# Hybrid layer on one core: delta-rule key factor by reciprocal, values' turns last, head norms run within the next head, memory K/V projected token-major with 512 moving columns

## The chip, the cores and the metric

The kernel runs on one core of a Trainium2 chip. The metric is the device time of one execution in microseconds (us); a kernel is run several times and the median is given. Engines are named as in the profile: PE multiplies matrices (PEld loads its stationary operand), DVE, ACT and POOL work on tiles, SP issues DMAs.

## What is computed

One step of a layer for 512 prompt tokens and 64 sample tokens (T = 576) with a model width of 1024. Everything is fp32, and the batches share the weights:

```python
h = x + concat(gdn, diff) @ w_out          # both from proj = rmsnorm(x) @ w_in
h = h + mem_attn(rmsnorm(h), mk, mv, w_mem_q, w_mem_o)
h = h + square(relu(rmsnorm(h) @ w_ff1)) @ w_ff2
y = rmsnorm(h)
# delta rule: k, q normed to length 1; chunks; unit lower triangular solve
ka = ka * rsqrt(sum(ka * ka) + EPS)
# diff attention, per head: two softmaxes, then a norm of the head's output
a = p[:, :, 0] - lam * p[:, :, 1]
ob = rmsnorm(a @ v, diff_norm) * (1 - lam_init)
# memory of the prompt: 256 tokens, 4 heads of 256
m = rmsnorm(mem, ln_mem_kv)
mk, mv = m @ w_mem_k, m @ w_mem_v          # both are outputs too
```

Outputs are y for both batches, the new keys and values of attention and memory, the delta rule's state and the convolution's last rows. The sample tokens use caches for the attention's and the memory's keys and values.

## The kernel before

**Products.** A large projection is done in a split format: x and w are each a high part in fp32r and a rest, and each product is three matmuls (wh·xh, wh·xl, wl·xh). `weights` (L141) loads 128 columns of a weight as raw tiles (three buffers), and ACT (L147) and DVE (L148) make `wh` and `wl` (two buffers each). `project` (L151) keeps a 128x128 piece of the weight stationary and moves 256 or 320 columns of the transposed activations through it; the result lies feature-major in one PSUM bank `pr` (three of them). The other banks are `ba` (two), `g0`, `g1` and `gs` (one each).

**Order.** A scheduler places the instructions on each engine by priorities that follow the program's order, and each engine runs its own list in order. Independent matmuls, here called filler, so come to stand between dependent ones: projections of the next stage within the delta rule and within the attention. A tile with few buffers is reused only when its readers are done.

**Stages.** The input projection and convolution; the delta rule in four chunks of 128 and one of 64; the attention, four heads with five query tiles each; the memory's K and V; `w_out`; the memory attention; the feed-forward layers `w_ff1` and `w_ff2`; the last norm.

**Delta rule.** `gdn_prep` prepares a chunk c with one bank, g0 or g1 by c's parity, through which everything goes in turn: the turns of the keys `bk` and of the queries `bq`; POOL's power of −1/2 of the sums of squares s8 (L527, `rpow` at L174); from it `nk` (L529), `brk` (L530, L531) and `rq2`; the turns `bv` of the values, scaled by `nk` into `vb` (L534 to L538); the decay `bg` (a matmul of `triu` and `gg`), the products `bkk` and `bkq`, and from L571 on the solve: `At` is made of `bkk`, `brk` and the decay, X is turned, and six levels of small products follow. `gdn_scan` then applies the chunk.

**Attention.** `diff_project` makes queries, keys and values of a head and writes the keys out through a staging tile `ko`, which shares its buffers with the probabilities `p0`. `diff_head` runs five query tiles (the sample's, t = 4, comes first). Behind them the head's norm: sums `so`, POOL's power `co` (L804), the product `an` on DVE (L805), five turns on PE, two scaled copies on ACT (L811) into `od`.

**Memory K/V (L824 to L844).** Eight weights each of 128 columns: feature-major products of 256 tokens, a copy, two turns, and copies into a staging tile `tm` (for K; it shares its buffers with `p1`), from which K goes out, or into `mv`.

**Row broadcast.** `norm_columns` gets a token's norm factor as a column (POOL's power at L884); `row_broadcast` (L176) turns the columns into rows by matmuls with the identity, and copies them to `rB`, which scales the results of the next projection.

## Time and profile before

| | |
|---|---|
| median of 3 runs | 1105.75 us (1105.25 to 1108.7) |
| profiled execution | 1104.43 us |
| its span | 1102.7 us |
| granted clock of PE, mean | 0.986 |
| stage 40 to 180 us: length, PE busy | 140.0, 134.82 us |
| stage 516 to 628 us: length, PE busy | 112.0, 108.66 us |
| DMA over the span | 90.62 MB, 82 GB/s |

The span runs from the first to the last instruction in the trace; what the execution takes besides is 1.7 us. In the views below a line such as `PE g L98 <- DVE vb L538` reads: PE, at an instruction of line 98 that writes a tile g, waited for DVE's writing (or reading) of `vb` at line 538. `pr<-u,wh 128*128 128x256` is an operation with its output, its inputs and its shapes; x3 is a count. Times of instructions on PE overlap, so what a matmul costs is the distance from one start to the next.

### The profile page before, as it was taken

The page shows a single profiled execution, that of the slowest core. Times are in us where ns is not written, and L with a number is a line of the kernel's source. Part 1 is how long each engine was busy: PE and PEld are TensorE (multiplying, and loading weights), DVE is VectorE, ACT ScalarE, POOL GpSimd, SP SyncE. Part 2 cuts the span into 40 slices and gives each one's busy share as a digit, 9 for nine tenths or more (in the row PEclk, how much of TensorE's full clock was granted, in tenths as well). Part 3 has the DMA queues.
Part 4 walks back from the last instruction along what each step waited for, and adds up shares of the span by engine and source line. Part 5 has one row for each costly group of instructions (what it writes and reads, how often), then busy time and mean ns, then how long its engine had stood idle before and what let it go on. Part 6 is the DMA issues. An engine that isn't in the chain of part 4 may idle for free.

```text
span 1102.7 us, 18954 instructions
## 1 busy us (share of the span) xinstructions
PE 1056.7 (96%) x7708; PEld 1002.8 (91%) x7708; DVE 623.8 (57%) x1335; ACT 408.4 (37%) x842; POOL 78.6 (7%) x127
## 2 busy tenths in 40 slices
PE   5999899899999999899999999999999999999997
PEld 5999799888888888799988799999999999999996
DVE  6766674665455566355454555655555555455554
ACT  5533554233135557543332343322222222222244
POOL 5421120221000000000000000000000000000000
PEclk9999999999999999899999999999999999999998
DMA  7242310100122254434211032223323141414122
GB/s 220 84 141 71 117 39 21 41 20 12 48 78 60 91 171 118 134 117 151 69 47 39 23 93 78 59 72 92 86 77 96 58 116 49 115 50 114 58 78 86
DMA packets 151494, 90.62 MB, mean 82 GB/s; under 512 B 5472, under 2 KB 147934, under 8 KB 150896
## 3 DMA queue, kind: packets, MB, share of 16 engines
q1 hardware_dynamic: 151408, 89.41, 27.6%
q8 instruction: 61, 1.00, 0.4%
q14 instruction: 25, 0.20, 0.1%
HBM read 79.66 MB, written 9.74 MB: 81 GB/s over the span
## 4 chain that ended last, share of the span: by engine, by line
issue 41%; PE 30%; DVE 1%; DMA 1%; ACT 1%; POOL 1%; POOLq 0%; ACTq 0%; SPq 0%
PE pr L98 20%; PE g L98 4%; PE ba L102 3%; PE gs L98 2%; PE ba L98 2%; DMA out_dram<-p 1%; POOL ta L174 0%; DVE an L805 0%; POOL tiny L174 0%; PE g L102 0%; DVE u L998 0%; ACT p L840 0%; DVE wl L148 0%; POOLq L1031 0%; ACT p L927 0%
## 5 line engine op out<-in xcount | busy, mean ns | idle before, releaser
L98 PE MATMUL pr<-u,wh 128*128 128x256 f32 (+1 forms) x3936 | 811.5, 300 | 0.4
L98 PEld LDWEIGHTS pr<-u,wh 128*128 128x128 f32 x3936 | 638.2, 191 | 7.0 <-issue 2.0
L98 PE MATMUL pr<-u,wl 128*128 128x256 f32 (+1 forms) x1968 | 584.9, 298 | 0.0
L98 PEld LDWEIGHTS pr<-u,wl 128*128 128x128 f32 x1968 | 373.2, 190 | 1.3 <-issue 0.2
L147 ACT CAST wh<-raw 128x1024 fp32r<-128x1024 f32 (+1 forms) x161 | 141.4, 878 | 289.0 <-PE pr L98 266.2
L148 DVE TENSOR_TENSOR wl<-raw,wh 128x1024 fp32r<-128x1024 f32 (+1 forms) x161 | 163.0, 1012 | 66.5 <-ACT wh L147 62.2
L858 DVE TENSOR_TENSOR u<-u,pr 128x256 f32<-128x256 f32 (+1 forms) x160 | 72.4, 453 | 105.2 <-PE pr L98 105.2
L964 DVE TENSOR_TENSOR p<-pr,rB 128x256 f32<-128x256 f32 x64 | 29.3, 458 | 65.4 <-PE pr L98 65.4
L167 ACT CAST u<-p 128x256 fp32r<-128x256 f32 x64 | 27.8, 434 | 89.2 <-DVE p L965 87.5
L174 POOL TENSOR_TENSOR tiny<-tiny,nhalf 128x1 f32<-128x1 f32 (+2 forms) x10 | 10.3, 1032 | 658.7 <-DVE tiny L882 488.3
L168 DVE TENSOR_TENSOR u<-p,u 128x256 fp32r<-128x256 f32 x64 | 29.2, 457 | 20.2 <-ACT u L167 20.2
L98 PE MATMUL g<-u,qz 128*128 128x256 f32 (+4 forms) x96 | 29.2, 405 | 1.2 <-ACT p L781 1.2
L965 DVE SCALAR_TENSOR_TENSOR p<-p 128x256 f32<-128x256 f32 x64 | 29.3, 458 | 1.7
L102 PE MATMUL ba<-ident,u 128*128 128x128 f32 (+2 forms) x128 | 22.7, 318 | 6.0 <-ACT p L840 3.2
L355 DVE SCALAR_TENSOR_TENSOR p<-p,gcol,p 128x579 f32<-128x579 f32 x33 | 27.1, 820 | 0.9
L98 PE MATMUL g<-Dt,B 128*128 128x128 f32 (+1 forms) x200 | 26.6, 278 | 0.9 <-DVE B L571 0.9
L571 DVE SCALAR_TENSOR_TENSOR B<-lev,At 128x512 f32<-128x512 f32 (+1 forms) x30 | 20.9, 708 | 10.0 <-PE g L98 6.9
L98 PEld LDWEIGHTS g<-Dt,B 128*128 128x128 f32 (+1 forms) x200 | 22.7, 185 | 4.0 <-ACT X L602 2.9
L781 ACT ACTIVATE p<-g,ta 128x320 f32<-128x320 f32 (+4 forms) x40 | 21.2, 532 | 13.6 <-DVE ta L779 10.4
L98 PE MATMUL g<-Y,X 128*128 128x128 f32 (+1 forms) x192 | 25.6, 274 | 0.2
L602 ACT COPY X<-g 128x512 f32<-128x512 f32 (+1 forms) x24 | 13.2, 549 | 33.7 <-PE g L102 33.6
L170 ACT ACTIVATE u<-u,gcol 128x256 fp32r<-128x256 f32 (+1 forms) x32 | 17.1, 533 | 23.1 <-DVE u L858 23.1
(270 smaller groups left out, 981.6 us busy)
## 6 DMA issues: line engine op xcount, KB each, us to landing
raw<-in_w_ff_dram SPq DMA_DIRECT2D x32, 512.0 KB
raw<-in_w_ff_dram SPq DMA_DIRECT2D x64, 256.0 KB
raw<-in_w_in_dram SPq DMA_DIRECT2D x28, 512.0 KB
raw<-in_w_mem_k_dram SPq DMA_DIRECT2D x8, 512.0 KB
raw<-in_w_mem_v_dram SPq DMA_DIRECT2D x8, 512.0 KB
raw<-in_w_out_dram SPq DMA_DIRECT2D x8, 512.0 KB
raw<-in_w_mem_q_dram SPq DMA_DIRECT2D x8, 512.0 KB
raw<-in_w_mem_o_dram SPq DMA_DIRECT2D x8, 512.0 KB
```

The lines of the kernel that those rows point to most:

```text
L98: nc.tensor.matmul(out, lhsT, rhs, start=start, stop=stop)
L102: nc.tensor.transpose(out, in_, ident[:n, :n])
L147: A.copy(wh, raw)
L148: V.tensor_tensor(wl, raw, wh.bitcast(F32), ALU.subtract)
L167: A.copy(h, src)
L168: V.tensor_tensor(lo, src, h.bitcast(F32), ALU.subtract)
L355: V.scalar_tensor_tensor(yv[:, :n], cb[:, i : i + n], cwt[:, m, i : i + 1], yv[:, :n], ALU.mult, ALU.add)
L571: V.scalar_tensor_tensor(B[:n, :, :n], lev[:n, :n].unsqueeze(1).to_broadcast([n, 4, n]), float(lv), At[:n, :, :n], ALU.is_equal, ALU.mult,)
L781: A.activation(p[:, :nk], b[:, :nk], AF.Exp, bias=mx[:, c : c + 1], scale=0.125, accum_out=l[:, c : c + 1])
L858: V.tensor_tensor(hm, hm, b, ALU.add)
L964: V.tensor_tensor(f, b, rB[:, a0 : a0 + n], ALU.mult)
L965: V.scalar_tensor_tensor(f, f, 0.0, f, ALU.max, ALU.mult)
```

## The change

There are four edits. (1) In `gdn_prep` the key factor `brk` is DVE's reciprocal of the sum of squares, times beta, in place of the square of POOL's power; `nk`, `rq2`, the turns of the values and `vb` move behind the product `KQ`. (2) `diff_head` returns its norm as a function `finish`, which the next head runs ahead of its third query tile, t = 1; the last head's runs behind the loop. (3) Memory K and V are made token-major: a 128x128 piece of the memory's tokens is stationary and 512 columns of the weight move, two banks `pr` for a block of 512 features; a raw tile holds 256 rows of the weight by 512 columns. Copies of DVE (tokens 0 to 127) and ACT (the rest) go to `mkt` (a tile of its own, unit 7) or `mv`, from which the outputs leave; only K is turned, from `mkt` into `mkT`. (4) The row broadcast runs between the two halves of the first projection that uses it, and two of its matmuls are kept in program order.

The diff, with most of its context left out; the end of it does to ff1 what is shown of the memory queries:

```diff
@@ -94,8 +94,10 @@
-    def mm(out, lhsT, rhs, start=True, stop=True):
-        nc.tensor.matmul(out, lhsT, rhs, start=start, stop=stop)
+    def mm(out, lhsT, rhs, start=True, stop=True, pin=False):
+        i = nc.tensor.matmul(out, lhsT, rhs, start=start, stop=stop)
+        if pin:
+            tc.keep_in_program_order(i)
@@ -138,17 +140,21 @@
 
-    def weights(w, c0, kt=KT):
-        raw = load(w, c0, kt)
-        wh = wp.tile([P, kt, P], F32R, tag="wh", name=nm("wh"))
-        wl = wp.tile([P, kt, P], F32R, tag="wl", name=nm("wl"))
+    def split_weights(w, shape):
+        raw = wp.tile(shape, F32, tag="raw", name=nm("raw"), bufs=3)
+        nc.sync.dma_start(raw, w.rearrange("(k p) n -> p k n", p=P))
+        wh = wp.tile(shape, F32R, tag="wh", name=nm("wh"))
+        wl = wp.tile(shape, F32R, tag="wl", name=nm("wl"))
         with tc.high_priority():
 
-    def project(w, x, evac, kt=KT, halves=HALVES):
+    def weights(w, c0, kt=KT):
+        return split_weights(w[:, c0 : c0 + P], [P, kt, P])
+    def project(w, x, evac, kt=KT, halves=HALVES, between=None):
 
@@ -158,6 +164,8 @@
+            if between and a0 == 0:
+                between()
@@ -173,16 +181,16 @@
 
-    def row_broadcast(rst, ntok, out):
+    def row_broadcast(rst, ntok, out, pin=False):
 
         for t in range(full):
-            mm(b[:, t * P : (t + 1) * P], bc(rst[:, t : t + 1], [P, P]), ident)
+            mm(b[:, t * P : (t + 1) * P], bc(rst[:, t : t + 1], [P, P]), ident, pin=pin and t == 0)
         A.copy(out[:, : full * P], b[:, : full * P])
             b2 = bank()
-            mm(b2[:, :DEC], bc(rst[:DEC, 4:5], [DEC, P]), ident[:DEC, :DEC])
+            mm(b2[:, :DEC], bc(rst[:DEC, 4:5], [DEC, P]), ident[:DEC, :DEC], pin=pin)
             V.tensor_copy(out[:, full * P :], b2[:, :DEC])
@@ -525,17 +533,9 @@
         rpow(r8[:n], s8[:n])
-        nk, brk, rq2 = tiny([P, 4], "tg"), tiny([P, 4], "tg"), tiny([P, 4], "tg")
-        V.tensor_tensor(nk[:n], s8[:n, 0:4], r8[:n, 0:4], ALU.mult)
-        V.tensor_tensor(brk[:n], r8[:n, 0:4], r8[:n, 0:4], ALU.mult)
+        brk = tiny([P, 4], "tg")
+        V.reciprocal(brk[:n], s8[:n, 0:4])
         V.tensor_tensor(brk[:n], brk[:n], beta[:n, c, :], ALU.mult)
-        V.tensor_scalar(r8[:n, 4:8], r8[:n, 4:8], P ** -0.5, None, ALU.mult)
-        V.tensor_tensor(rq2[:n], r8[:n, 4:8], r8[:n, 4:8], ALU.mult)
-        bv = bank(f"g{c % 2}")
-        for h in range(H):
-            tr(bv[:n, h * P : (h + 1) * P], cv_[:, h, L])
-        vb = sb("vb")
-        V.tensor_tensor(vb[:n], v4(bv, P)[:n], nk[:n].unsqueeze(2).to_broadcast([n, 4, P]), ALU.mult)
 
@@ -560,6 +560,15 @@
         V.tensor_tensor(KQ[:n, :, :n], v4(bkq, n)[:n], gam[:n, :, :n], ALU.mult)
+        nk, rq2 = tiny([P, 4], "tg"), tiny([P, 4], "tg")
+        V.tensor_tensor(nk[:n], s8[:n, 0:4], r8[:n, 0:4], ALU.mult)
+        V.tensor_scalar(r8[:n, 4:8], r8[:n, 4:8], P ** -0.5, None, ALU.mult)
+        V.tensor_tensor(rq2[:n], r8[:n, 4:8], r8[:n, 4:8], ALU.mult)
+        bv = bank(f"g{c % 2}")
+        for h in range(H):
+            tr(bv[:n, h * P : (h + 1) * P], cv_[:, h, L])
+        vb = sb("vb")
+        V.tensor_tensor(vb[:n], v4(bv, P)[:n], nk[:n].unsqueeze(2).to_broadcast([n, 4, P]), ALU.mult)
         if c > 0:
@@ -754,13 +763,15 @@
 
-    def diff_head(h):
+    def diff_head(h, between):
 
         for t in (4, 0, 1, 2, 3):
+            if t == 1:
+                between()
             q0 = QT[t][0]
@@ -800,48 +811,62 @@
             A.copy(on[:, t, :], po)
-        V.tensor_scalar(so, so, 1.0 / P, EPS, ALU.mult, ALU.add)
-        rpow(co, so)
-        V.tensor_tensor(on, on, co.unsqueeze(2).to_broadcast([P, 5, P]), ALU.mult)
-        b, b2 = bank(), bank()
-        for t in range(4):
-            tr(b[:, t * P : (t + 1) * P], on[:, t, :])
-        tr(b2[:, :P], on[:, 4, :])
-        for src, ts_ in ((b, slice(0, SEQ)), (b2[:, DEC:P], slice(SEQ, T))):
-            A.activation(od[:, h, ts_], src, AF.Identity, scale=dn)
+        def finish():
+            V.tensor_scalar(so, so, 1.0 / P, EPS, ALU.mult, ALU.add)
+            rpow(co, so)
+            V.tensor_tensor(on, on, co.unsqueeze(2).to_broadcast([P, 5, P]), ALU.mult)
+            b, b2 = bank(), bank()
+            for t in range(4):
+                tr(b[:, t * P : (t + 1) * P], on[:, t, :])
+            tr(b2[:, :P], on[:, 4, :])
+            for src, ts_ in ((b, slice(0, SEQ)), (b2[:, DEC:P], slice(SEQ, T))):
+                A.activation(od[:, h, ts_], src, AF.Identity, scale=dn)
+        return finish
+    finish = lambda: None
     for h in range(H):
             diff_cache()
-        diff_head(h)
+        finish = diff_head(h, finish)
+    finish()
 
 
-    mxs = ([mh[:, 0:4, :], mh[:, 4:8, :]], [ml[:, 0:4, :], ml[:, 4:8, :]])
     mkT = unit(2, [P, KT, NMEM])
     mv = unit(3, [P, 2, D])
-    for w, out in ((w_mem_k, o_mk), (w_mem_v, o_mv)):
-        for m in range(KT):
-            d = mkT[:, m, :] if out is o_mk else small("zr", [P, 320])[:, :NMEM]
-            project(weights(w[0], m * P), mxs, lambda b, a0, n: A.copy(d, b), halves=((0, NMEM),))
-            b = bank()
-            for bi in range(2):
-                tr(b[:, bi * P : (bi + 1) * P], d[:, bi * P : (bi + 1) * P])
+    mkt = unit(7, [P, 2, D])
+    for w, dst, out in ((w_mem_k, mkt, o_mk), (w_mem_v, mv, o_mv)):
+        for f in range(2):
+            fs = slice(512 * f, 512 * f + 512)
+            bs = [bank("pr") for _ in range(2)]
+            for kc in range(4):
+                wt = split_weights(w[0, 256 * kc : 256 * kc + 256, fs], [P, 2, 512])
+                for k in (2 * kc, 2 * kc + 1):
+                    for t in range(2):
+                        ts_ = slice(t * P, (t + 1) * P)
+                        for j, (wi, x) in enumerate(((0, mh), (0, ml), (1, mh))):
+                            mm(
+                                bs[t], x[:, k, ts_], wt[wi][:, k % 2, :],
+                                start=(k == 0 and j == 0), stop=(k == KT - 1 and j == 2),
+                            )
+            for t in range(2):
+                (A.copy if t else V.tensor_copy)(dst[:, t, fs], bs[t])
             if out is o_mk:
-                if m % 2 == 0:
-                    tm = small("tm", [P, 2, 256])
-                dst = tm[:, :, (m % 2) * P : (m % 2 + 1) * P]
-            else:
-                dst = mv[:, :, m * P : (m + 1) * P]
-            A.copy(dst, b[:, :256].rearrange("p (b n) -> p b n", b=2))
-            if out is o_mk and m % 2:
-                nc.sync.dma_start(out[0, 0, :, m // 2, :].rearrange("(b p) d -> p b d", p=P), tm)
-        if out is o_mv:
-            nc.sync.dma_start(out[0, 0].rearrange("(b p) h d -> p b (h d)", p=P), mv)
+                for i in range(2):
+                    b = bank()
+                    for j in range(2):
+                        m = 4 * f + 2 * i + j
+                        for t in range(2):
+                            tr(b[:, j * 256 + t * P : j * 256 + (t + 1) * P], dst[:, t, m * P : (m + 1) * P])
+                    m = 4 * f + 2 * i
+                    A.copy(mkT[:, m : m + 2, :], b.rearrange("p (j n) -> p j n", j=2))
+            nc.sync.dma_start(out[0, 0].rearrange("(b p) h d -> p b (h d)", p=P)[:, :, fs], dst[:, :, fs])
 
@@ -890,7 +915,8 @@
-    rB = row_broadcast(norm_columns(), T, const([P, T], "rB"))
+    cols, rB = norm_columns(), const([P, T], "rB")
+    broadcast = lambda: row_broadcast(cols, T, rB, pin=True)
@@ -912,6 +938,7 @@
+                between=broadcast if h == i == 0 else None,
...
```

Instructions stand in each engine's list in a fixed order. Three places are shown with names that carry the tiles' numbers.

First PE's list in chunk 2 of the delta rule. Names with g0 are chunk 2's bank in its turns, g1 is chunk 1's or 3's; u_103 are the values, u_74 the queries, `pr` is filler. Before:

```order
L102 MATMUL g0_313_2072<-ident_80,u_103_862 128x128 x2
L98 MATMUL pr_513_2949<-u_7_94,wl_509_2914 128x320
L98 MATMUL pr_513_2949<-u_7_94,wh_508_2913 128x320
L98 MATMUL pr_513_2949<-u_9_96,wh_508_2913 128x320
L98 MATMUL pr_513_2949<-u_7_94,wl_509_2914 128x320
L98 MATMUL pr_513_2949<-u_7_94,wh_508_2913 128x320
L98 MATMUL pr_513_2949<-u_9_96,wh_508_2913 128x320
L98 MATMUL gs_356_2248<-on_355_2246,X_242_1646 128x128 x4
L102 MATMUL g1_366_2291<-ident_80,u_48_328 128x128
L98 MATMUL g0_315_2079<-triu_91,gg_1208 128x128 x4
```

Now, at the same decay matmul:

```order
L104 MATMUL g0_308_2054<-ident_80,u_74_577 128x128 x4
L98 MATMUL pr_506_2884<-u_8_95,wl_504_2854 128x320
L98 MATMUL pr_506_2884<-u_8_95,wh_503_2853 128x320
L98 MATMUL gs_354_2241<-S_298_2024,u_48_328 128x128 x2
L98 MATMUL g0_311_2067<-triu_91,gg_1208 128x128 x4
L98 MATMUL gs_354_2241<-S_298_2024,u_48_328 128x128 x2
L98 MATMUL pr_506_2884<-u_10_97,wh_503_2853 128x320
```

The matmul of `triu` and `gg` into g0 followed the turns of the values (u_103); it now follows those of the queries (u_74), and the values come later in the list.

Second, DVE's list at the same place. tg_303 is POOL's power, tg_304 the sums of squares, Y0 the decay, At0 the system. Before:

```order
L526 TENSOR_SCALAR tg_304_2043<-tg_304_2043 128x8
L529 TENSOR_TENSOR tg_310_2064<-tg_304_2043,tg_303_2042 128x4
L530 TENSOR_TENSOR tg_311_2065<-tg_303_2042 128x4
L532 TENSOR_SCALAR tg_303_2042<-tg_303_2042 128x4
L538 TENSOR_TENSOR vb_314_2077<-g0_313_2072,tg_310_2064 128x512
L531 TENSOR_TENSOR tg_311_2065<-tg_311_2065,beta_1209 128x4
L533 TENSOR_TENSOR tg_312_2066<-tg_303_2042 128x4
L634 TENSOR_TENSOR vn_357_2253<-gs_356_2248,tg_231_1599 128x512
L545 TENSOR_SCALAR Y0_316_2084<-g0_315_2079,Gc_1248 128x128 x4
L656 TENSOR_REDUCE tg_360_2273<-on_362_2275 128x4
L555 SCALAR_TENSOR_TENSOR At0_318_2096<-g0_317_2091,tg_311_2065,Y0_316_2084 128x128 x4
```

Now:

```order
L533 TENSOR_REDUCE tg_304_2043<-B0_309_2059 128x4
L534 TENSOR_SCALAR tg_304_2043<-tg_304_2043 128x8
L537 RECIPROCAL tg_310_2064<-tg_304_2043 128x4
L564 TENSOR_TENSOR tg_317_2096<-tg_304_2043,tg_303_2042 128x4
L565 TENSOR_SCALAR tg_303_2042<-tg_303_2042 128x4
L538 TENSOR_TENSOR tg_310_2064<-tg_310_2064,beta_1209 128x4
L545 TENSOR_SCALAR Y0_312_2072<-g0_311_2067,Gc_1248 128x128 x4
L566 TENSOR_TENSOR tg_318_2097<-tg_303_2042 128x4
L638 TENSOR_TENSOR on_355_2246<-vb_240_1640,gs_354_2241 128x512
L730 COPY qz0_2844<-pr_506_2884 64x320
```

Before, `nk` (L529) and the factor `brk` (L530, L531) and `vb` stood ahead of the decay (L545). Now the reciprocal (L537) stands ahead of `nk` (L564), and the product with beta (L538) and the decay (L545) stand behind it; `vb` has left this piece.

Third, PE's list at the end of the last head. `an` is the head's output; u_800 is `mkT` before, u_802 is `mkt` now; zr is a piece of V before its turn. Before:

```order
L98 MATMUL pr_874_4839<-u_149_1288,wh_872_4835 128x256
L98 MATMUL pr_874_4839<-u_148_1287,wl_873_4836 128x256
L102 MATMUL ba_796_4367<-ident_80,an_750_4206 128x128 x4
L102 MATMUL ba_797_4368<-ident_80,an_750_4206 128x128
L102 MATMUL ba_806_4420<-ident_80,u_800_4386 128x128 x2
L102 MATMUL ba_812_4457<-ident_80,u_800_4386 128x128 x2
L102 MATMUL ba_817_4494<-ident_80,u_800_4386 128x128 x2
L102 MATMUL ba_823_4531<-ident_80,u_800_4386 128x128 x2
L102 MATMUL ba_828_4568<-ident_80,u_800_4386 128x128 x2
L102 MATMUL ba_834_4605<-ident_80,u_800_4386 128x128 x2
L102 MATMUL ba_839_4642<-ident_80,u_800_4386 128x128 x2
L102 MATMUL ba_845_4679<-ident_80,u_800_4386 128x128 x2
```

Now:

```order
L98 MATMUL pr_820_4479<-wh_828_4518,u_148_1287 128x512
L98 MATMUL pr_820_4479<-wh_828_4518,u_149_1288 128x512
L98 MATMUL pr_820_4479<-wl_829_4519,u_148_1287 128x512
L104 MATMUL ba_796_4367<-ident_80,an_748_4194 128x128 x4
L104 MATMUL ba_797_4368<-ident_80,an_748_4194 128x128
L98 MATMUL pr_819_4478<-wh_828_4518,u_148_1287 128x512
L98 MATMUL pr_819_4478<-wh_828_4518,u_149_1288 128x512
L98 MATMUL pr_819_4478<-wl_829_4519,u_148_1287 128x512
L104 MATMUL ba_817_4465<-ident_80,u_802_4388 128x128 x4
L104 MATMUL ba_818_4471<-ident_80,u_802_4388 128x128 x4
```

Before, the turns of `an` were followed by eleven pairs of turns of K and V with no product between them. Now products of 512 columns stand ahead of and behind `an`, and the turns of K come behind three more of them. Of the memory's sixteen weights, PE's list had thirteen ahead of these turns of `an`; it now has six and a half.

More of the change, by code (lines that the diff above doesn't have):

```diff
@@ L953, in hybrid_layer_kernel @@
         project(weights(w_mem_o[0], m * P), (moh, mol), add_residual(m, True, (fh, fl), G_FF))
-    rB = row_broadcast(norm_columns(), T, const([P, T], "rB"))
+    cols, rB = norm_columns(), const([P, T], "rB")
+    broadcast = lambda: row_broadcast(cols, T, rB, pin=True)
     NG = 8
@@ L966, in evac @@
                 split_to((sh, sl), f, i, a0)
-            project(weights(w_ff1[0], (4 * g + i) * P), (fh, fl), evac)
+            project(
+                weights(w_ff1[0], (4 * g + i) * P), (fh, fl), evac, between=broadcast if g == i == 0 else None
+            )
         return sh, sl
```

## The prediction

> **What bounds the kernel now.** I read the page's busy times first, then the table of stages, then who waited for whom on TensorE.
>
> ```profile
> PE 1056.7 (96%) x7708; PEld 1002.8 (91%) x7708; DVE 623.8 (57%) x1335; ACT 408.4 (37%) x842; POOL 78.6 (7%) x127
> 180.00:310.00 130.00, 122.37 (x974) 109.20 (x972) 72.56 (x166) 38.52 (x71) 21.37 (x18) 0.99 0.11 30
> 310.00:448.00 138.00, 131.29 (x921) 116.68 (x919) 85.25 (x244) 78.62 (x233) 5.55 (x7) 1.00 0.37 111
> 448.00:456.00 8.00, 4.52 (x20) 3.01 (x21) 0.76 (x1) 3.97 (x14) 0.00 (x0) 0.68 0.60 197
> 678.00:1085.00 407.00, 406.77 (x3048) 406.58 (x3049) 226.91 (x427) 111.64 (x181) 0.18 (x1) 1.00 0.27 77
> ```
>
> TensorE (PE) is busy for 96% of the span and no other engine for more than 57%. In the stage table each row has the stretch, its length, then the busy time of PE, PEld, DVE, ACT and POOL, the clock, the DMA share and GB/s. The feed-forward stage (678 to 1085 us) has no gap at all, so nothing is won there without removing matmuls. The gaps lie in the delta rule (to 310), the attention (to 448) and the eight microseconds behind it. So the change can pay in two ways: less work on PE, or shorter waits in these three stages.
>
> ```profile
> PE g L98 <- DVE vb L538: 7.7, 5, 2.3
> PE ba L102 <- ACT p L840: 3.2, 3, 2.5
> ```
>
> These are two rows of PE's waits (total, times, longest), and an edit is about each: the values' turns, and the copies that follow the memory projection.
>
> **Memory projection: the matmuls.** 384 matmuls with 256 moving columns become 192 with 512, and 16 of the transposes `ba<-ident,zr` go. The price of a matmul is the distance between starts, since durations overlap:
>
> ```profile
> 459.81 0.28 PE L98 MATMUL pr<-u,wl 128*128 128x256 f32 x1
> ...
> 460.53 0.28 PE L98 MATMUL pr<-u,wl 128*128 128x256 f32 x1
> ...
> 799.79 0.31 PE L98 MATMUL pr<-u,wl 128*128 128x320 f32 x1
> ...
> 800.67 0.31 PE L98 MATMUL pr<-u,wl 128*128 128x320 f32 x1
> ```
>
> Between the first two starts stand six matmuls of 256 columns: 0.72/6 = 120 ns each. Between the last two stand six of 320: 0.88/6 = 147 ns. So 64 more columns cost 27 ns, 0.42 ns each, and 512 columns come to 147 + 192 × 0.42 = 227 ns by the line through both. The bounds are 213 ns (0.42 per column and nothing fixed) and 240 ns (twice the 256). 384 × 0.120 = 46.1 us becomes 192 × 0.227 = 43.6 us: **−2.5 us** (−5.2 to 0). For the transposes the row of five at 445.79, below, has 0.74 us; about 0.11 us each, so 16 × 0.11: **−1.8 us**. The 24 fewer copies of ACT lie beside PE's work and count nothing, except at the places below.
>
> The Trainium skill, page "TensorE: Matmul & The Clock Gate", section "Back-to-back issue gap", gives about 131 ns per matmul for a sustained stream at N=512. That is less than the 147 ns which this trace shows for only 320 columns, so I don't use it in the sum; by it the 192 would be 25 us, 21 less than now, which is the last of the rivals.
>
> **Memory projection: the hole behind the last head.** The chain there, in order of time (start, length, what), with the clock beside it:
>
> ```profile
> 443.18 1.61 POOL ta L174
> 444.81 0.83 DVE an L805
> 445.65 0.14 issue
> 445.79 0.64 PE ba L102 x4
> 446.45 0.90 ACT u L811 x2
> 447.38 0.67 ACT u L167
> 448.05 0.55 ACT p L840 x2
> 448.62 3.37 DMA out_dram<-p
> ...
> 452.09 0.38 ACT p L840
> 450.90:457.80 6.90, 4.89 (x21) 4.00 (x22) 0.00 (x0) 3.63 (x12) 0.00 (x0) 0.51 0.41 141
> ```
>
> The last head's norm (pow on POOL, product on DVE) ends at 445.65; then eleven waiting pairs of turns of K and V go through two `ba` banks and ACT copies, and at 448.62 a copy must wait 3.37 us until the staging tile `tm` has been written out. PE stands idle for 8.00 − 4.52 = 3.5 us from 448 on and for about 1 us ahead of it (while ACT empties the banks of `an`, 0.90 us), and the clock falls to 0.51 for 6.9 us with 4.89 us of work in it, which at full clock is 2.5 us. Together 7.0 us.
>
> Afterwards there is no `tm`, no transpose of V, and the output leaves from a tile that nobody waits for, so the 3.37 us have no successor. The last norm remains: POOL 1.6, DVE 0.8, and the `so` ahead of them, some 3.3 us behind the last `gs`. In the new order 11 matmuls of 512 (11 × 0.227 = 2.5 us) stand between that `gs` and the transposes of `an`, so about 0.8 us stays bare. Without the idle stretch I expect no fall of the clock. 7.0 − 0.8: **−6.2 us** (−7 if all is covered; −2 if the clock still falls and K's transposes wait for their copies).
>
> A new cost: every 512-column block takes two of three `pr` banks, so the next block's second group waits for a copy. A 512-column copy from PSUM takes 0.59 us on ACT:
>
> ```profile
> L602 ACT COPY X<-g 128x512 f32<-128x512 f32 x20 | 11.7, 586 | 26.5 <-PE g L102 26.4
> L148 DVE TENSOR_TENSOR wl<-raw,wh 128x1024 fp32r<-128x1024 f32 x97 | 118.7, 1223 | 63.9 <-ACT wh L147 61.8 <-DMA raw<-in_w_mem_k_dram 1.1 <-PE ba L102 0.7
> L147 ACT CAST wh<-raw 128x1024 fp32r<-128x1024 f32 x97 | 101.7, 1048 | 153.7 <-PE pr L98 130.9 <-issue 17.5 <-POOL cst L359 2.2
> ```
>
> PE has 0.68 us of other work (three matmuls); the copy hides, unless DVE or ACT is in one of its 1.0 to 1.2 us splits just then. Three such turns at 0.5 us: **+1.5 us** (0 to 3.5). The split of a weight (1.05 + 1.22 = 2.3 us) still fits beside the other buffer's 12 × 0.227 = 2.7 us, with 0.4 us to spare; before it was 24 × 0.120 = 2.9.
>
> **Delta rule: the values' turns.** The wait as it stands, chunk 1:
>
> ```profile
> 132.82 1.65 POOL L174 TENSOR_TENSOR tg<-tg,nhalf 128x8 f32<-128x8 f32 x1 [3.52 <-DVE tg L526]
> 136.57 1.77 PE L98 MATMUL g<-triu,gg 128*128 128x128 f32 x8 [2.28 <-DVE vb L538]
> 136.90:140.30 3.40, 3.40 (x17) 3.40 (x16) 1.52 (x6) 0.00 (x0) 0.56 (x1) 0.50 0.00 0
> 215.40:218.80 3.40, 3.40 (x17) 3.40 (x17) 1.49 (x3) 0.91 (x3) 0.16 (x1) 0.51 0.17 48
> L783 DVE RECIPROCAL ta<-ta 128x2 f32<-128x2 f32 x20 | 3.2, 159 | 11.6 <-ACT p L781 11.5
> ```
>
> The transposed values hold the bank g1 until DVE has scaled them into `vb`; that needs `nk`, which needs POOL's power of 1.65 us. PE is in order, and the decay matmul that wants the bank stands at its head. After the idle 2.28 us the clock is at 0.50 for 3.4 us, which costs 1.7 us more. In the new order `bg` follows the queries' turns, whose only reader is ACT's square, and `brk` comes from DVE's reciprocal (0.16 us in the last row). So all five waits go: **−7.7 us**. The delta rule has a second fall of the clock, at 215.4 us, behind another kind of wait; I take the first alone: **−1.7 us** (0 to −3.4).
>
> What is late next? Two things.
>
> ```profile
> L174 POOL TENSOR_TENSOR tg<-tg,nhalf 128x8 f32<-128x8 f32 x4 | 6.6, 1646 | 41.5 <-DVE tg L526 41.5
> L538 DVE TENSOR_TENSOR vb<-g,tg 128x512 f32<-128x512 f32 x4 | 2.8, 692 | 0.0
> ```
>
> First, DVE is in order too, and in chunk 2 the new order puts `nk` (which waits for POOL) ahead of `brk`'s product and of the decay's four subtractions: there the 1.65 us is moved to the chain that ends in `At`. In the other chunks `brk` and decay stand ahead of `nk`. Second, `bv` now holds the bank between KQ and the turn of At, so 0.69 us of `vb` comes into each chunk's chain. That is 1.65 + 5 × 0.69 = 5.1 us at most; filler of PE covers part, and I take 3.4: **+3.4 us**. Sum of the edit **−6.0 us** (−11 to 0).
>
> On the clock, the Trainium skill, same page, section "Part 1: The HAM clock gate", puts the fall to half after an idle window of about 3.4 us. Here 2.28 us of idleness was enough, and the row decides; by the rule the fall would have another cause and the 1.7 us would stay.
>
> **Attention: the head norms.** The row of the turns, and a wait on POOL:
>
> ```profile
> L102 PE MATMUL ba<-ident,an 128*128 128x128 f32 x20 | 3.0, 278 | 3.1 <-DVE ta L779 1.8 <-DVE an L805 1.3
> POOL p L788 <- DMA out_dram<-p: 20.5, 3, 11.0
> ```
>
> PE idles 3.1 us ahead of the twenty transposes of `an`; 0.3 of it lies ahead of the last head's and is counted above. Run behind the next head's first two tiles, three of the four norms have several microseconds of cover: **−2.8 us**. But the attention also loses filler. Before, 13 of the 16 memory weights (2.9 us of matmuls each) stand in PE's order ahead of the last head's `an`; in the new order six and a half (2.7 us each), so some 20 us of the 131 busy ones leave for the time behind it. Twenty tiles then share 111 us, 5.6 each. How fast tiles alone could run no row shows; it lies between DVE's 85.25/20 = 4.3 us, if its work never waits, and the 138/20 = 6.9 us at which they run now with the filler. POOL's fill of `p0` waits up to 11.0 us for the keys' output DMA, and the deferred pow is queued behind it on POOL. I give back 3 us: **0 us** (−3 to +8; the nearest measured row is the 7 us of gaps that 310 to 448 already has).
>
> **Row broadcast.** The place where PE waits for it:
>
> ```profile
> 523.98 1.52 PE L98 MATMUL ba<-ident,tiny 128*128 128x128 f32 x10 [0.77 <-POOL tiny L174]
> ```
>
> For the memory queries the broadcast moves behind further matmuls: **−0.8 us** (−1.2 to 0). For ff1 the order leaves it where it was: 0.
>
> **Sum.** −2.5 − 1.8 − 6.2 + 1.5 − 6.0 + 0 − 0.8 = **−15.8 us**. The profiled execution took 1104.4 us (span 1102.7), 1.3 below the median 1105.75. 1104.4 − 15.8 = 1088.6, and 1.3 above it for a median: 1089.9, call it **1090 us**. A measurement can tell 0.3% (3.3 us) from no change.
>
> **Rivals.**
> - *The attention becomes bound by its chains.* With 20 us less filler, PE waits for the tiles. For it: 5.6 us of work per tile lies in the middle of 4.3 to 6.9, and the 11.0 us wait for the keys' DMA, which for head 3 stands right behind the reload of `hd` in SP's queue. Against it: DVE and ACT are at 85 and 79 us of 138. At 6.1 us a tile, 20 × 0.5 = +10: **1100 us**.
> - *The values' turns don't do what they say.* POOL's pow is awaited by `nk` on DVE in every chunk, and the chain behind `vb` is bare. Speaks for it: chunk 2's order. Against: four other chunks. The −6.0 becomes 0: **1096 us**. With the first rival together, 1106, no change.
> - *Slower: a 512-column matmul in this split format runs like plain f32.* One row has plain f32 at 512 columns:
>
> ```profile
> L98 PE MATMUL g<-p,u 128*128 128x512 f32 x16 | 8.1, 605 | 0.0
> L98 PE MATMUL pr<-u,wh 128*128 128x256 f32 x2096 | 399.0, 288 | 0.2
> ```
>
>  The split format's duration is 288 against a distance of 120, 168 ns more; so plain f32 takes 605 − 168 = 437 ns at 512. 192 × 0.437 = 83.9, 37.8 us above now instead of 2.5 below: 1090 + 40 = **1130 us**. It turns slower than before from about 0.31 us a matmul. Against it: 320 columns cost nearly in proportion.
> - *The distance stops growing above 320 columns*, so that 512 cost the same 147 ns: 192 × 0.147 = 28.2, 15.4 less than the 43.6 of the sum, **1075 us**. The step from 256 to 320, 27 ns for 64 columns, speaks against it. The Trainium skill's sustained figure (the page and section above) is of this kind.
>
> **How the numbers follow.** Forecast (1080 to 1095): 0.55. Attention rival alone 0.16, values' turns alone 0.14, both together 0.07, the slower one 0.06, the short matmul 0.02. The range leaves out the last three and takes in the first three with their terms' ends: low 1078 (5 below for the delta rule's end of −11, 2.7 for the matmuls', 3 for the norms', 0.8 for the hole's), high 1101. Faster by over 0.3%: 0.87; within: 0.07; slower: 0.06.
>
> **What would show it.** Right: no row of PE waiting for `vb`; the clock at 1.0 behind the last head; 192 matmuls of 512 columns with starts 227 ns apart; memory stage without gaps beyond 1 us. Wrong: gaps of PE ahead of `aT` or `p` in the attention (first rival), ahead of the turns of At with DVE waiting for POOL at `nk` (second), or a distance above 0.31 us (third). A stall of the dense V projections on the split of their weights, for which I have only 0.4 us a weight to spare, would make the forecast wrong by 16 times what is missing.

## The result, and the profile after

The changed kernel takes 1079.13 us (median of 4 runs, 1078.14 to 1079.84) against 1105.5 us before (4 runs, 1104.23 to 1108.7). The ratio is 0.9757 (95% interval 0.9734 to 0.9779): 2.4% faster, 26 us, where 16 were forecast. The time lies within the stated range, near its fast end, and just outside the forecast's own 1080 to 1095.

First the busy times on the page of the changed kernel, then its table of stages, cut at the places that answer to those of before (the delta rule ends at 302 us, the last head at 414, the memory's projection at 443):

```profile
PE 1045.9 (97%) x7500; PEld 986.4 (92%) x7500; DVE 626.5 (58%) x1339; ACT 403.2 (37%) x818; POOL 80.1 (7%) x127
```

```profile
180.00:302.00 122.00, 117.24 (x938) 104.18 (x938) 72.61 (x167) 37.64 (x70) 21.40 (x18) 1.00 0.12 32
302.00:414.00 112.00, 110.84 (x690) 93.68 (x688) 74.35 (x233) 67.90 (x214) 6.21 (x7) 1.00 0.35 107
414.00:443.00 29.00, 28.78 (x138) 23.74 (x139) 15.56 (x16) 14.29 (x19) 0.00 (x0) 1.00 0.66 198
443.00:494.00 51.00, 51.00 (x385) 51.00 (x384) 27.95 (x51) 20.97 (x40) 0.00 (x0) 1.00 0.37 106
```

In the attention PE now idles 1.2 us of 112 (before 6.7 of 138), and the stretch behind it, where V is projected almost without company, has 0.2 us of idleness in 29. The clock is at 1.0 in both. What PE still waits for, cut to the rows used below (total, times, longest):

```profile
PE g L104 <- DVE vb L571: 2.6, 2, 1.6
PE g L98 <- DVE At L555: 1.9, 1, 1.9
...
PE gs L98 <- DVE on L638: 1.2, 1, 1.2
...
PE ba L104 <- DVE an L818: 1.0, 1, 1.0
...
PE ba L98 <- POOL tiny L182: 0.8, 1, 0.8
```

For an account by stages I take PE's start-to-start distances apart: work is the number of matmuls times the distance of their kind when nothing is missing (120, 147 and 227 ns for 256, 320 and 512 columns, 109 for a turn), and a gap is all beyond that, idle time and slow clock alike. The stages go from one landmark on PE to the next, since filler moved between them; `vs` are the values of the sample tokens, with which each head's first query tile ends.

| from, to | work before, after | gaps before, after |
|---|---|---|
| start, chunk 0's decay | 108.5, 104.9 | 17.2, 16.0 |
| chunk 0's decay, head 0's first product with `vs` | 159.3, 157.0 | 37.3, 31.7 |
| that, head 3's first product with `vs` | 85.5, 70.7 | 11.4, 5.9 |
| that, `w_out` | 32.9, 49.7 | 9.8, 2.4 |
| `w_out`, `w_mem_o` | 134.7, 134.5 | 8.3, 7.1 |
| all the kernel | 996.0, 991.9 | 97.1, 76.3 |

Work fell by 4.1 us; the gaps by 20.8: 6.8 in the first two stages, 5.5 in the attention, 7.4 at its end, 1.2 in the memory's attention.

### The profile page after: what moved, and what is told of

It is laid out like the page before. It is cut to its first block, busy times and chain, and to the rows that moved or that the text cites. A ratio compares the mean times of both kernels' runs of the same rounds, so it can differ in the third digit from the quotient of the medians.

```text
span 1077.3 us, 18494 instructions
## 1 busy us (share of the span) xinstructions
PE 1045.9 (97%) x7500; PEld 986.4 (92%) x7500; DVE 626.5 (58%) x1339; ACT 403.2 (37%) x818; POOL 80.1 (7%) x127
## 3 DMA queue, kind: packets, MB, share of 16 engines
q1 hardware_dynamic: 138848, 89.41, 28.1%
## 4 chain that ended last, share of the span: by engine, by line
PE 51%; issue 42%; DVE 4%; POOL 2%; DMA 1%; ACT 1%; POOLq 0%; SPq 0%; DVEq 0%; ACTq 0%
PE pr L98 32%; PE g L98 9%; PE ba L104 3%; PE gs L98 3%; PE ba L98 2%; PE g L104 2%; POOL tg L182 1%; DMA raw<-in_w_in_dram 1%; POOL tiny L182 1%; DVE B L580 1%; DVE u L210 0%; DVE u L257 0%; DVE wl L150 0%; DVE Dt L607 0%; POOL u L576 0%
## 5 line engine op out<-in xcount | busy, mean ns | idle before, releaser
L98 PE MATMUL pr<-u,wh 128*128 128x256 f32 (+1 forms) x3680 | 759.2, 300 | 0.1
L98 PEld LDWEIGHTS pr<-u,wh 128*128 128x128 f32 x3680 | 596.8, 190 | 5.0 <-issue 2.4
L98 PE MATMUL pr<-u,wl 128*128 128x256 f32 (+1 forms) x1840 | 548.8, 300 | 0.0
L98 PEld LDWEIGHTS pr<-u,wl 128*128 128x128 f32 x1840 | 348.5, 190 | 1.8 <-issue 0.7
L182 POOL TENSOR_TENSOR tiny<-tiny,nhalf 128x1 f32<-128x1 f32 (+2 forms) x10 | 10.7, 1071 | 666.3 <-DVE tiny L907 495.7
L98 PE MATMUL pr<-wh,u 128*128 128x512 f32 x128 | 42.0, 404 | 0.0
L98 PEld LDWEIGHTS pr<-wh,u 128*128 128x128 f32 x128 | 23.4, 188 | 4.5 <-issue 0.2
L98 PE MATMUL pr<-wl,u 128*128 128x512 f32 x64 | 25.6, 400 | 0.0
```

The source lines that it names most:

```text
L98: i = nc.tensor.matmul(out, lhsT, rhs, start=start, stop=stop)
L182: G.tensor_tensor(out, in_, bc(nhalf[: in_.shape[0], 0:1], list(in_.shape)), ALU.pow)
```

## The experiments

Twelve variants ran against the kernel before; the last one puts the two fastest together. Medians of before in these comparisons are 1105.8 to 1106.4 us, so a difference between two kernels from different comparisons is uncertain by about 1 us. "Undone" kernels have three of the four edits, "only" kernels have one.

| kernel | us, median | ratio to before (95%) |
|---|---|---|
| undo_turns | 1087.41 | 0.9833 (0.9819 to 0.9846) |
| undo_norms | 1086.97 | 0.9823 (0.9809 to 0.9836) |
| undo_mem | 1085.63 | 0.9815 (0.9801 to 0.9828) |
| undo_bcast | 1079.18 | 0.9758 (0.9745 to 0.9771) |
| only_norms | 1094.23 | 0.9893 (0.9880 to 0.9907) |
| only_mem | 1106.42 | 1.0001 (0.9992 to 1.0010) |
| late_pow | 1081.23 | 0.9773 (0.9760 to 0.9787) |
| recip_early | 1087.65 | 0.9824 (0.9801 to 0.9846) |
| mem256 | 1081.83 | 0.9788 (0.9769 to 0.9806) |
| bv_ba | 1073.66 | 0.9718 (0.9699 to 0.9736) |
| later | 1077.19 | 0.9748 (0.9730 to 0.9766) |
| both | 1071.89 | 0.9693 (0.9680 to 0.9706) |

### Each edit undone

The first four take one part of the diff back and leave the rest; their edits are the parts of the diff above, reversed.

> The changed kernel, with the delta rule's part as it was before (key factor from POOL's power, values' turns ahead of the decay). Theory: the waits for vb and the clock's fall come back, and the delta rule gets 6 to 8 us longer: 1085 to 1087 us, with five waits of 1.2 to 2.5 us ahead of the matmul of triu and gg. Rival (the gain in this stretch is owed to filler that the memory's projection moved): less than 2 us longer, 1079 to 1081 us.

8.3 us longer. PE's waits in its delta rule are those of before, to the tenth of a microsecond:

```profile
PE g L98 <- DVE vb L546: 7.7, 5, 2.3
```

The theory holds for the waits; filler that others moved is not the cause.

> The changed kernel, with each head's norm run at the head's own end as before. Theory: the 5.5 us that the attention gained come from the deferred norms, so four waits of about 1 us ahead of the turns of an come back, and the time is 3 to 5 us longer: 1082 to 1084 us. Rival (they come from the memory's projection, which took the staging tile tm off the buffers of p1 and its copies off ACT): at most 1 us longer.

7.8 us longer, more than the theory asked for. The gaps of the attention are 10.7 us in place of 5.9, and those from head 3's first product to `w_out` 4.8 in place of 2.4. The waits from 314 to 450 us:

```profile
PE ba L104 <- DVE an L814: 2.8, 3, 1.0
PE g L98 <- ACT p L790: 1.5, 1, 1.5
PE ba L104 <- DVE ta L788: 0.9, 1, 0.9
```

The first and third rows are the four waits ahead of the turns of `an`, 3.7 us (the third names what DVE did last, not what was awaited). The rest is the second row and the clock, which here fell between 404 and 412 us too.

> The changed kernel, with the memory's K and V projected feature-major with 256 moving columns as before. Theory by terms: 4.3 us of work on PE and the hole behind the last head (6 us) come back: 10 us longer, 1089 us. Rival (the memory's projection also gave the attention its 5.5 us): 15 us longer, 1094 us. Rival (the hole came from the last head's norm alone and the deferral closes it): 5 us longer.

6.5 us longer, between the figures of two of the theories. By the stage account 4.1 of it are work and 2.2 are gaps at the end of the attention (4.6 in place of 2.4); the attention itself is as short as in the changed kernel (5.9). So the attention's gain isn't the memory's. And the hole behind the last head does not come back. This is all PE waits for between 314 and 450 us:

```profile
PE ba L104 <- DVE an L818: 1.2, 1, 1.2
PE g L98 <- ACT p L792: 0.2, 1, 0.2
```

The old memory code, with its staging tile `tm`, its turns of V and its copies, is all there, and neither PE nor ACT waits for its output DMA.

> The changed kernel, with the row broadcasts run ahead of the projections as before. Theory: only the wait of POOL ahead of the memory queries comes back: 1.0 us longer, 1080 us, and nothing at ff1. Rival (the pinned matmuls had costs elsewhere): no difference or faster.

No difference in time (1079.18 against 1079.13). In the trace the gaps between `w_mem_q` and `w_mem_o` are 7.6 us in place of 6.9; 0.7 us is less than these medians can show.

### Two edits alone

> The kernel before, with the deferred head norms as its only edit. Theory (the hole behind the last head is made by the norm that stands ahead of the memory's turns in PE's list, so that deferring alone closes most of it): about 5 us in the attention and 5 us behind it, 10 us faster than before, 1096 us. Rival (my prediction's reading: the hole belongs to the memory's copies and its staging tile): 3 to 5 us faster, and the gap of over 2 us at the wait for the output DMA is still there.

12.1 us faster than before, a little more than the theory. Gaps of the attention 6.1 (before 11.4), of its end 4.4 (before 9.8). Deferring the norm closes the hole by itself: between 328 and 458 us PE waits for `an` (1.2 us), `aT` (0.6) and `ta` (0.3) and for no copy of the memory's.

> The kernel before, with the token-major memory K and V as its only edit. Theory (it too closes most of the hole, so the two edits overlap): 4 us of work and 5 us of the hole, 9 us faster than before, 1097 us. Rival (the hole is the norm's alone): 4 us faster, 1102 us.

No change at all, which neither side expected. The memory's edit does save its 4.1 us of work and 4.2 of the gaps at the end (5.6 in place of 9.8, and part of the 5.6 is a fall of the clock from 424.5 to 431.3 us that began in the attention). The hole is gone here too, though the norm stands at the head's own end: from 430 us to the start of `w_out` PE waits once, 1.1 us for `an`. But the attention's gaps grow from 11.4 to 21.6 us. Waits of PE in this kernel from 329 to 471 us:

```profile
PE ba L104 <- DVE ta L787: 5.0, 4, 2.9
PE g L98 <- ACT p L789: 2.3, 2, 1.2
PE gs L98 <- ACT aT L801: 2.2, 4, 0.7
PE ba L104 <- DVE p L794: 2.1, 2, 1.2
```

The longest of them, at the end of head 2, in order of time, with lines between left out, and the clock behind it:

```profile
411.95 1.16 PE L98 MATMUL gs<-u,aT 128*128 128x128 f32 x8 [0.67 <-ACT aT L801]
...
413.54 0.17 DVE L811 TENSOR_SCALAR ta<-ta 128x5 f32<-128x5 f32 x1 [3.04 <-ACT p L809]
...
413.80 1.17 POOL L182 TENSOR_TENSOR ta<-ta,nhalf 128x5 f32<-128x5 f32 x1 [23.47 <-DVE ta L811]
415.00 0.82 DVE L813 TENSOR_TENSOR an<-an,ta 128x640 f32<-128x640 f32 x1 [0.89 <-POOL ta L182]
...
415.97 1.30 PE L104 MATMUL ba<-ident,an 128*128 128x128 f32 x5 [2.86 <-DVE ta L787]
```

```profile
416.00:420.00 4.00, 3.44 (x15) 2.83 (x16) 0.55 (x3) 2.30 (x7) 0.00 (x0) 0.50 0.04 13
```

The last product of head 2 ends at 413.1, the norm's turns begin at 415.97, and in between PE has nothing: the chain of square, POOL's power and DVE's product stands bare for 2.9 us, and the clock, which falls at 414.3 within it, is at half behind it. This is the first rival of the prediction, at work. The work between the landmarks is 74.8 us in place of 85.5, so the filler that hid such chains has gone. With the norms deferred the work there is only 70.7 us, and yet the gaps are 5.9: the chain that needed the filler is no longer waited for.

### The delta rule's edit taken apart

```diff
 late_pow:
-        V.reciprocal(brk[:n], s8[:n, 0:4])
+        V.tensor_tensor(brk[:n], r8[:n, 0:4], r8[:n, 0:4], ALU.mult)
 recip_early: the lines from nk, rq2 = ... to vb stand ahead of bg again
```

> The changed kernel, with the values' turns late but the key factor again from the square of POOL's power. Theory (what counted was PE's order, the decay takes longer than the power): within 1 us of the changed kernel, 1078 to 1080 us. Rival (the reciprocal counted, since the factor of At would wait for POOL): 1.65 us in each of five chunks, some 5 to 8 us longer, 1084 to 1087 us.

2.1 us longer than the changed kernel, nearer to the theory than to the rival, and outside the 1 us of the theory. The runs of the two do not overlap (1080.85 to 1081.38 against 1078.14 to 1079.84), but the size is known to about 1 us. Among the waits in its delta rule are two that grew or came:

```profile
PE g L98 <- DVE At L555: 2.1, 1, 2.1
...
PE g L98 <- DVE Y L545: 0.9, 1, 0.9
```

> The changed kernel, with the reciprocal but the values' turns ahead of the decay as before. Theory (PE's order counted): the waits for vb come back, 6 to 8 us longer than the changed kernel, 1085 to 1087 us, as with the whole edit undone. Rival (the reciprocal counted): within 2 us of the changed kernel.

8.5 us longer, as much as the whole edit undone (8.3). The order of the turns on PE is worth some 6 us, the reciprocal some 2 on top of it, and without the order nothing. One of the five runs of this kernel is far from the others, and with it the mean clock that was granted:

```
us     1087.57  1088.14  1089.10  1081.27  1087.65
clock    0.989    0.988    0.988    0.998    0.988
```

### The matmuls, and two ways on

The edits, cut to their main lines (`later` also moves the split of `od` behind the memory's loop):

```diff
 mem256:
+                            for q in (slice(0, 256), slice(256, 512)):
-                                bs[t], x[:, k, ts_], wt[wi][:, k % 2, :],
+                                bs[t][:, q], x[:, k, ts_], wt[wi][:, k % 2, q],
 bv_ba:
-        bv = bank(f"g{c % 2}")
+        bv = bank()
 later: in project
             if between and a0 == 0:
-                between()
+                done.append((b[:, :n], a0, n))
+                continue
+            if between:
+                between()
+            for d in done:
+                evac(*d)
 later: in the memory's loop, ahead of V
+            if out is o_mv and f == 0:
+                finish()
```

> The changed kernel, with each 512-column matmul of the memory's projection made as two of 256 (the same results, 384 matmuls again). Theory (a matmul costs 13 ns beside its columns): 384 x 0.120 against 192 x 0.227, 2.5 us longer, 1081.6 us. Rival (512 columns have no advantage of their own, or the pitch is not what bounds there): within 1 us of the changed kernel. Rival (512 columns are much faster than in proportion): over 5 us longer.

2.7 us longer, and 2.5 us of work in the stage account of its trace. The distance itself stands in the changed kernel's timeline (start, length, what):

```profile
424.81 0.39 PE L98 MATMUL pr<-wl,u 128*128 128x512 f32 x1
...
428.89 0.39 PE L98 MATMUL pr<-wl,u 128*128 128x512 f32 x1
```

Eighteen matmuls lie between these starts: 4.08/18 = 227 ns.

> The changed kernel, with the turns of the values in a bank of the pair ba in place of the chunk's own bank. Theory (the bank that waits for vb still holds up the turns of X): the two waits for vb, 2.6 us in all, go; 1 to 3 us faster, 1076 to 1078 us. Rival (DVE's chain behind is late anyway, or ba is then missed elsewhere): no difference or slower.

5.5 us faster than the changed kernel, twice what was expected. This is what it removes; in the changed kernel, chunk 2:

```profile
205.33 0.69 DVE L580 SCALAR_TENSOR_TENSOR B<-lev,At 128x512 f32<-128x512 f32 x1 [1.18 <-POOL u L576]
205.94 0.68 DVE L571 TENSOR_TENSOR vb<-g,tg 128x512 f32<-128x512 f32 x1
...
206.68 0.66 PE L104 MATMUL g<-ident,X 128*128 128x128 f32 x4 [1.65 <-DVE vb L571]
```

The turns of X wait for the bank that the values hold until `vb` is made, which waits behind `B` on DVE, which waits for POOL. With the values in a bank `ba`, PE waits for `vb` nowhere in the delta rule; the waits left there, the longest three:

```profile
PE gs L98 <- DVE on L670: 2.4, 3, 0.9
PE g L98 <- DVE At L555: 1.9, 1, 1.9
PE g L98 <- DVE B L580: 0.9, 2, 0.5
```

Gaps are 28.1 us in place of 31.7 there and 4.3 in place of 5.9 in the attention. This profile has no fall of the clock at 136 us, which the changed kernel's has; that is not the edit's doing (the last section shows it), and up to 1.7 us of the difference between the two profiles are owed to it.

> The changed kernel, with the last head's norm behind the memory's K, and the row broadcasts behind both halves of the first projection (its results are scaled after that). Theory: the wait of 1.2 us ahead of the last turns of an and that of 0.9 us at ff1 go, 2 us faster, 1077 us. Rival (the waits move: to K's turns, or to the banks pr that the two halves hold): no difference.

1.9 us faster than the changed kernel by the medians, at the limit of what they show; the trace bears it out. In its profile PE waits no more for `an` or for POOL, and its gaps are 1.5 us in place of 2.4 ahead of `w_out` and 1.3 in place of 2.4 in the first half of the feed-forward stage.

> The changed kernel with the two edits of bv_ba and later together: the values' turns in a bank ba, the last head's norm behind the memory's K, the row broadcasts behind both halves. Theory (they lie in different stages and add): 1079.1 - 5.5 - 1.9, 1072 us, with none of the waits for vb, for the last an and for POOL at ff1. Rival (the two both use ba, or the clock's falls made part of one of them): only the better of the two, 1074 us.

1071.89 us, 3.1% faster than before and 0.7% faster than the changed kernel, as the theory has it: the two add. Among PE's waits in its profile there is none for `vb`, for `an` or for POOL at ff1.

## Why the prediction was right, and where its sizes were off

**The matmuls (−2.5) and the turns (−1.8): right.** 227 ns was predicted from two shapes and 227 was measured; work fell by 4.1 us where 4.3 were predicted, and making the 512 columns two times 256 costs 2.7. Neither of the rivals about the distance (437 and 147 ns) came; plain fp32 itself takes 429 ns from start to start at 512 columns in both traces, so the 437 worked out from durations was near. (To the nanosecond the line through the two shapes gives 228.) The Trainium skill's 131 ns (page "TensorE: Matmul & The Clock Gate", section "Back-to-back issue gap") does not hold for this format; its isolated figure in the same section, N/2.4 + 2.5 ns or 216 for 512 columns, is 5% below the 227 of the trace.

**The delta rule (−6.0): right in size; what came back was only in part what was named, and the clock's term was luck.** The waits ahead of the decay are gone, all 7.7 us. PE's waits from 100 us to the end of the delta rule fell from 12.8 to 8.0 us, by 4.8 where −7.7 + 3.4 makes 4.3; gaps fell by 6.8 including the stretch ahead of chunk 0's decay, and 8.3 us is what undoing the edit costs.

Of the 3.4 us that were to come back, `vb` at the turns of X is 2.6, in two chunks and not in all five, so that the prediction's first sign of being right (no row of PE waiting for `vb`) was not met, against its own second term. Chunk 2's order is there as well, with 1.2 us: `nk` waits for POOL, and what stands behind it on DVE comes late, though it is not `At` that PE then waits for but `on`:

```profile
193.70 0.17 DVE L564 TENSOR_TENSOR tg<-tg,tg 128x4 f32<-128x4 f32 x1 [1.55 <-POOL tg L182]
...
195.03 0.68 DVE L638 TENSOR_TENSOR on<-vb,gs 128x512 f32<-128x512 f32 x1
...
195.76 1.16 PE L98 MATMUL gs<-on,X 128*128 128x128 f32 x8 [1.21 <-DVE on L638]
```

The wait of 1.9 us for `At` was in no term. It is chunk 0's, and POOL's power is in it too, by POOL's own list:

```profile
130.32 0.63 ACT L548 ACTIVATE Y<-Y 128x512 f32<-128x512 f32 x1
...
131.55 1.65 POOL L182 TENSOR_TENSOR tg<-tg,nhalf 128x8 f32<-128x8 f32 x1 [1.95 <-DVE tg L534]
...
133.16 1.28 POOL L549 TENSOR_TENSOR Y<-Y,triu 128x512 f32<-128x512 f32 x1
...
134.48 1.13 DVE L555 SCALAR_TENSOR_TENSOR At<-g,tg,Y 128x128 f32<-128x128 f32 x4 [2.10 <-POOL Y L549]
```

Chunk 0's decay leaves ACT at 130.95, but POOL's list has chunk 1's power ahead of the product with `triu` that the decay still needs, and so `At` starts at 134.48 and PE's next product at 135.66. No run moved that power, so what it is worth is open. The reciprocal by itself is worth some 2 us.

The −1.7 for the clock came true by luck. The fall at 136.9 that was to go stayed (now at 136.2, behind the wait for `At`), and the one at 215.4 that was to stay went:

```profile
136.00:140.00 4.00, 4.00 (x22) 3.96 (x21) 3.85 (x5) 1.07 (x2) 1.81 (x2) 0.57 0.00 0
```

**The attention (0 predicted, −5.5 measured): the step that was most off.** It was "I give back 3 us" for the filler that leaves. The mechanism is real, only_mem shows 10 us of it; but what the thinner filler had left bare was above all the chain of the norm, and this very chain the change takes off PE's path. POOL's wait for the keys' output DMA, feared there, did grow, to 23.4 us, and no wait of PE came of it. I summed the two edits as if they stood side by side, and the measured −5.5 lies outside the −3 to +8 that this term was given. Deferring is worth 7.8 us with the other edits in place and 12.1 without them, and the memory's edit 6.5 with the deferral and nothing alone.

**The hole behind the last head (−6.2, and +1.5 for the banks): right that it closes, and the cause named is one of two that each suffice.** The prediction had it close because `tm` and V's turns go, and only_mem, with the norm still at the head's own end, has no hole. But undo_mem keeps the old memory code, and there is no hole either; only_norms closes it by itself as well. So the hole needs both: the old code of the memory and a norm whose turns stand ahead of that code's turns. The end of the attention has gaps of 9.8 us with both, 4.4 and 5.6 with one edit alone, 2.4 without either. I read it so: PE's list is in order, the eleven pairs of turns stood behind the waiting `an`, and came through two banks all at once; the wait for the DMA only followed from the crowd. That either edit closes it is shown; the crowding as its way is argued from the order. The bare rest of the last norm was predicted at 0.8 us; it is 1.0 us of idleness, 1.2 by the distances, at the end of this chain:

```profile
409.75 0.92 PE gs L98 x8
...
410.70 0.58 DVE u L176
...
411.37 0.18 DVE ta L816
...
411.62 1.61 POOL ta L182
...
413.25 0.84 DVE an L818
...
414.22 0.74 PE ba L104 x5
```

The +1.5 us for the turns of the banks `pr` was mis-sized: it is nothing, as the 0.2 us of idleness from 414 to 443 us show. Nor did the dense V projections stall on the split of their weights, which I had feared.

**The row broadcast (−0.8): too small to show in the time;** in the trace it is there with 0.7 us, and ff1's wait stayed as predicted until `later` moved it.

The sum therefore fell short by 5.5 us in the attention and by 2.7 at the hole and the banks, of the 9.6 between 15.8 and the 25.4 by which the profiled span shrank; the delta rule and the broadcast add 1.2. The clock's falls are within these gaps: between 40 and 600 us the trace before has three, one of them long, and the one after has one. That 1079 still lies in the stated range is in part luck: the range's low end, 1078, was made mostly of 5 us for the delta rule and 2.7 for the matmuls, which came out near their middle, and allowed 3.8 for the two terms that gave 5.5 and 2.7 more.

## What to carry to other kernels

A matmul that waits for a slow chain costs by what stands behind it in the in-order list, so look there first: moving the waiting instruction one block later paid more here than taking work away, and it closed a hole that looked as if it belonged to the memory's copies alone. Filler is worth something only while a bare chain is there to be hidden; edits that thin the filler and edits that defer the chain must be priced together, since one of them can be worth nothing alone (only_mem) and much beside the other: only_norms and only_mem gain 12.1 and 0 us, while undo_turns, which has both and the row broadcast, gains 18.8. Where one bank or buffer is handed down a chain of uses, a slow reader in the middle should get another one: a one-word edit (`bv_ba`) was worth 5.5 us.

## What the runs showed of the hardware

The clock of PE falls to half, for 3.4 us or 6.8, after gaps of only about 2 us, and not after each of them. Where the gap lies decides. Within a trace the falls begin whole multiples of 3.41 us apart (before: 136.9, 215.4 and 451.0, which is 23 and 69 steps), as if the clock were decided once in each step. The wait of 1.86 us ahead of `At` stands in the changed kernel and in bv_ba, on PE and then in the clock's column (the last but two):

```profile
135.66 1.15 PE L98 MATMUL g<-u,u 128*128 128x128 f32 x6 [1.86 <-DVE At L555]
135.85 0.82 PE L98 MATMUL g<-u,u 128*128 128x128 f32 x5 [1.86 <-DVE At L555]
136.00:140.00 4.00, 3.52 (x27) 3.32 (x27) 3.93 (x6) 2.36 (x3) 1.82 (x2) 1.00 0.00 0
```

In the changed kernel (first row; its clock is shown above, 0.57) PE is idle from 133.80 to 135.66, all within one step, 132.82 to 136.23, and the clock falls at its end. In bv_ba (the other rows) it is idle from 133.99 to 135.85; counted from the falls of its own trace, at 25.1 and 1059.3, a step ends in between, at 134.29, and the clock stays. Nine of the traces have this wait (1.85 to 2.08 us). In the four where it lies within one step (after, undo_norms, late_pow, later) the clock falls, and in the five with a step's end inside it (undo_mem, undo_bcast, mem256, bv_ba, both) it stays. So whether a gap of this size costs 1.7 us more is a matter of phase. The 2.28 us ahead of the fall at 136.9 in the kernel before lie within one step as well.

One program (recip_early), run five times, had a mean clock of 0.988 or 0.989 four times and 0.998 once, and that run was some 6 us shorter than the others. Only one of the longer four was traced; it has 3.4 us at half clock from 137 us and 6.8 us from 267, which costs some 5 us, so that the falls are the likely reason, but not a shown one. The mean clock alone does not tell the time: the traced run of `both` has 0.946, with 0.95 on record over nearly its whole length, was only 1.8 us longer than the median, and its matmuls of 256 and 512 columns still start 120 and 227 ns apart. The Trainium skill says (page "TensorE: Matmul & The Clock Gate", section "Part 1: The HAM clock gate") that the window is free-running and that its effect differs from run to run; these traces and runs agree, with the numbers above.
